# The sample stream's products with the old mLSTM memory: unsplit fp32, one key block per strip of 32 PSUM partitions

## The chip, the cores and the metric

The kernel runs on one core of one Trainium2 chip. The metric is the device time of one execution in microseconds (us). The time of a kernel is the median of its runs. Beside them one execution is profiled; times of single instructions, waits and windows come from that execution, counted from the start of its span.

## The reference

One layer of a streaming encoder is computed for a prompt of 512 frames and for a sample of 32 frames that continues a running stream. Two branches, an mLSTM with 4 heads of width 512 and an HGRN2 with 8 heads of width 128, are merged by gates and projected. The change lies in the mLSTM, in the term that reads the old matrix memory `C`, which only the sample has:

```python
s = jnp.einsum('bhtd,bhsd->bhts', q, k) * dmat
num = w_inter[..., None] * jnp.einsum('bhed,bhtd->bhte', C, q) + jnp.einsum('bhts,bhse->bhte', s, v)
den = w_inter * jnp.einsum('bhd,bhtd->bht', n, q) + jnp.sum(s, axis=-1)
h = num / jnp.maximum(jnp.abs(den), jnp.exp(-m_t))[..., None]
C_new = decay[..., None, None] * C + jnp.einsum('bhs,bhse,bhsd->bhed', w_last, v, k)
```

For the sample of one head, `num` is the product of 32 weighted queries (512 long) with a 512 x 512 memory, plus the 32 x 32 scores times the values. The kernel keeps the normaliser `n` as further columns of the memory, so that numerator and denominator come out of the same products, 516 columns wide (`VW`), in two halves of 258 (`VH`).

## The kernel before, in words

**Products.** Nearly all products are made from split operands: a value is stored as a high part in fp32r (a copy on ScalarE, ACT in the profile) and the rest as a low part (a subtraction on VectorE, DVE), and high x high, high x low and low x high are summed in PSUM. TensorE (PE) runs at one pass per such product. A few small products are left unsplit in fp32, those of the HGRN2 chain among them (L1511, L1606, L1630 to L1634).

**Order.** PE executes in the order in which the code is written. A generator `mchain(h, pump)` holds one mLSTM head's chain; at each `yield` it lets the `Pump` issue some of the products of the input projection (L370, L485), so that PE has work while the chain's results are copied. The orders of ACT and DVE are made by a scheduler from readiness and priority when the program is built; `tc.high_priority()` raises what it encloses. GpSimd (POOL) does small copies, SyncE (SP) issues loads and stores.

**One head in mchain.** Keys and values are transposed, weighted and split: `kw[b]` (high and low) and `vv[b]` for the four prompt blocks b, `kws` and `vs` for the sample. The old memory is loaded into `c0[f]`, f = 0 to 3 for the key blocks of 128 (L950). Then, in the order in which PE meets it:

- `old(f)` splits `c0[f]` into `c0h` and `c0l` (L956 on ACT, L957 on DVE).
- Heads 0 to 2: `memory(h, f, ...)` makes the prompt's new memory for f = 0 to 3, 24 products each (tile `C`, L902), and ACT copies each result out in two pieces (`Co`, L914). Behind each of them stands one `new_memory` product (tile `Cs`, L1004), which DVE merges into `c0` (L1006). In head 3 the operands are stored to `kv_d` instead, and the prompt's memory is made at the end of the program.
- The numerators `nm` of the prompt blocks i = 0 to 3 (L1077: 6, 12, 18 and 24 products), with the other `new_memory` products between them. Each result is copied out by ACT (`y`, L1088).
- Ahead of the last block, `sample()`: 16 split products with the old memory (L1054) and two with the scores (`dss`, L1051). The queries' high and low parts stand side by side in `qw`, so that PSUM partitions 0 to 31 receive the high and 32 to 63 the low part's sum; ACT copies the two out (L1063, L1065) and DVE adds them (L1066).

**Buffers.** The PSUM tiles of `paux` (`vt`, `vts`, `C`, `nm`, `yt`) come from a pool of two buffers, of two banks each. A new tile takes a buffer when the last reader of its former tile is done. `Cs` tiles come from another pool (`pd`) of four, which the projection shares. In SBUF there are 22 slots "s" and 12 slots "e" for tiles of 550 columns; `kw`, `vv` and the `y` tiles live in "s".

Of the kernel before, what the change touches and what calls it, by code (L numbers as in the profile page):

```python
# [9 lines left out]
F32 = mybir.dt.float32  # L10
F32R = mybir.dt.float32r
# [3 lines left out]
ALU = mybir.AluOpType  # L15
AX = mybir.AxisListType

P = 128
D = 1024
KD = D // P  # L20
NS = 32
# [5 lines left out]
KH = HD // P  # L27
HH = 8
NB = NP // P
VW = HD + 4  # L30
# [34 lines left out]
def hybrid_step(ctx: ExitStack, tc: tile.TileContext, a, o):  # L65
# [12 lines left out]
    def slot(name, dt=F32):  # L78
        return sp.tile([P, SLOT], dt, tag="s", name=name)
# [5 lines left out]
    def small(name, shape, dt=F32, bufs=2, tag=None):  # L85
        return tp.tile(shape, dt, tag=tag or name, name=name, bufs=bufs)

    def two(ap):
        return ap.rearrange("p (a b) -> p a b", a=2)
# [8 lines left out]
    def paux(name):  # L98
        return pa.tile([P, 2, 512], F32, tag="a", name=name)
# [724 lines left out]
    def stage_q(h, u):  # L824

        t = st8[h]
        if u == 0:
            t.update(qs=[], qf=small("qf", [P, KH * NS]), qw=small("qw", [P, KH, 2, NS], F32R))
        with tc.high_priority() if u and not h else nullcontext():
            w = t.pop("wq", None) or weight(a["w_qm"][h, u], f"wq{h}{u}")  # L830
        for f in range(2):
            acc = dense(w, f * P, 256, P, t["cs"], f"q{h}{u}{f}")
            i = u * 2 + f
            qh, ql = [eslot(f"q{n}{h}{i}", F32R) for n in "hl"] if h else pair_tile(f"q{i}", 1)
            S.copy(t["qf"][:, i * NS : (i + 1) * NS], acc[0][:, :NS])
            for b in range(2):
                with tc.high_priority():
                    read = S.copy(qh[:, half(b)], acc[b])
                    low = V.tensor_tensor(ql[:, half(b)], acc[b], qh[:, half(b)].bitcast(F32), ALU.subtract)
            t["qs"].append((qh, ql))  # L840
        if u:

            with tc.issue_after(read.ins):
                S.activation(small("silu", [1, 2]), ident[:1, :2], AF.Silu)
        return low

    def stage_scores(h):

        dj, ds, wi, ks, ksm, qs, qf, qw = (st8[h][k] for k in ("dj", "ds", "wi", "ks", "ksm", "qs", "qf", "qw"))
        for i in range(KH):  # L850
            qt = small("qt", [P, NS])
            G.tensor_tensor(qt, qf[:, i * NS : (i + 1) * NS], wi, ALU.mult)
            G.tensor_copy(qw[:, i, 0], qt)
            G.tensor_tensor(qw[:, i, 1], qt, qw[:, i, 0].bitcast(F32), ALU.subtract)
        sh2, sl2 = slot(f"sh2{h}", F32R), slot(f"sl2{h}", F32R)
        st = []
        for j in range(NB):
            pn = paux(f"sc{h}{j}")
            n = NP - j * P
            for f in range(KH):  # L860
                for i, (x, y) in enumerate(((0, 0), (0, 1), (1, 0))):
                    PE.matmul(  # L862
                        pn[:, 0, :n],
                        ks[f][x][:, j * P : (j + 1) * P],
                        qs[f][y][:, NS + j * P : T],
                        start=(f == 0 and i == 0),
                        stop=(f == KH - 1 and i == 2),
                    )
            with tc.high_priority():
                V.tensor_tensor(dj[j], pn[:, 0, :n], dj[j], ALU.mult)  # L870
            if j < 2:
                sh, sl = slot(f"sh{h}{j}", F32R)[:, :n], slot(f"sl{h}{j}", F32R)[:, :n]
            else:
                sh, sl = (x[:, (j - 2) * 256 : (j - 2) * 256 + n] for x in (sh2, sl2))
            with tc.high_priority():
                S.copy(sh, dj[j])  # L876
                low = V.tensor_tensor(sl, dj[j], sh.bitcast(F32), ALU.subtract)
            st.append((sh, sl))
        pn = paux(f"scs{h}")
        for f in range(KH):  # L880
            PE.matmul(
                pn[: 3 * NS, 0, :NS],
                ksm[:, f],
                qf[:, f * NS : (f + 1) * NS],
                start=(f == 0),
                stop=(f == KH - 1),
            )
        dss = small("dss", [3 * NS, NS], F32R)
        V.tensor_tensor(ds, pn[: 3 * NS, 0, :NS], ds, ALU.mult)
        V.tensor_copy(dss, ds)  # L890
        V.tensor_tensor(dss[2 * NS :], ds[2 * NS :], dss[2 * NS :].bitcast(F32), ALU.subtract)
        st8[h].update(st=st, dss=dss)
        return low
# [26 lines left out]
    def mchain(h, pump):  # L920
# [28 lines left out]
        for f in range(KH):  # L949
            nc.sync.dma_start(c0[f][:, :VW], a["C0"][h, f])  # L950

        def old(f):
            new = eslot if f < 2 else slot
            ch, cl = new(f"c0h{h}{f}", F32R), new(f"c0l{h}{f}", F32R)
            with tc.high_priority():
                S.copy(ch[:, :VW], c0[f][:, :VW])  # L956
                V.tensor_tensor(cl[:, :VW], c0[f][:, :VW], ch[:, :VW].bitcast(F32), ALU.subtract)  # L957
            return ch, cl


        if h:
            yield max(0, max(pump.when["v", f] for f in range(KH)) - pump.done)
        vt = t["vt"]
# [31 lines left out]
                for k in (1, 2):  # L995
                    xf[k] = xf_sums(k)
        yield 4
        olds = [old(0), old(1)]

        def new_memory(f, g):  # L1000

# [6 lines left out]
                nc.sync.dma_start(o["Cs"][h, f], c0[f][:, :VW])  # L1008

        parts = [(f, g) for f in range(KH) for g in range(2)]  # L1010
        if h == MH - 1:

            for b in range(NB):
                for i in range(2):
                    nc.sync.dma_start(kv_d[b, i, :, :HD], kw[b][i][:, :HD].bitcast(F32))
                    nc.sync.dma_start(kv_d[NB + b, i, :, :VW], vv[b][i][:, :VW].bitcast(F32))
        else:
            for f in range(KH):
                for _ in memory(h, f, kw, vv):
                    pass  # L1020
                new_memory(*parts.pop(0))


        st, dss, qw = (t[k] for k in ("st", "dss", "qw"))
        stt = small("stat", [P, NB + 1, 2])
        den = small("den", [P, NB + 1])
        emc = small("emc", [P, NB + 1])
# [6 lines left out]
        def numbers(i, p, y):  # L1034
            bs = small("bs", [P, 6])
            V.bn_stats(bs[:p], y[:p, :HD])  # L1036
            V.bn_aggr(stt[:p, i, :], bs[:p])
            V.tensor_copy(den[:p, i : i + 1], y[:p, HD : HD + 1])

        yb = []  # L1040
        olds += [old(2), old(3)]

        def sample():
            pn = paux(f"nm{h}{NB}")
            for f in (0, 1, 3, 2):
                ch, cl = olds[f]
                last = f == 2
                for g in range(2):
                    v = slice(g * VH, (g + 1) * VH)
                    if last:  # L1050
                        PE.matmul(pn[:NS, g, :VH], dss, vs[:, v], start=False, stop=False)  # L1051
                    both, low = (4 if last or f == 0 else 2, 0), (1, 1)
                    for m, x in (low, both) if last else (both, low):
                        PE.matmul(  # L1054
                            pn[: m * NS, g, :VH],
                            qw.rearrange("p f o t -> p (f o t)")[:, 2 * f * NS : (2 * f + m) * NS],
                            (ch, cl)[x][:, v],
                            start=(f == 0 and x == 0),
                            stop=(last and x == 0),
                        )  # L1060
            ysm = slot(f"y{h}{NB}")
            with tc.high_priority():
                S.copy(two(ysm[:, :VW]), pn[:, :, :VH])  # L1063
                yl = slot(f"yl{h}")
                S.copy(two(yl[:NS, :VW]), pn[NS : 2 * NS, :, :VH])  # L1065
                V.tensor_tensor(ysm[:NS, :VW], ysm[:NS, :VW], yl[:NS, :VW], ALU.add)  # L1066
                numbers(NB, NS, ysm)
            return ysm

        for i in range(NB):  # L1070
            if i == NB - 1:
                ysm = sample()
            pn = paux(f"nm{h}{i}")
            for j in range(i + 1):
                for q, (x, y) in enumerate(((0, 0), (0, 1), (1, 0))):
                    for g in range(2):
                        PE.matmul(  # L1077
                            pn[:, g, :VH],
                            st[j][x][:, (i - j) * P : (i - j + 1) * P],
                            vv[j][y][:, g * VH : (g + 1) * VH],  # L1080
                            start=(j == 0 and q == 0),
                            stop=(j == i and q == 2),
                        )
                if parts and i and (h == MH - 1 or i > 1):
                    new_memory(*parts.pop(0))
            y = slot(f"y{h}{i}")
            with tc.high_priority():
                S.copy(two(y[:, :VW]), pn[:, :, :VH])  # L1088
                numbers(i, P, y)
            yb.append(y)  # L1090
# [795 lines left out]
```

## Time and profile before

| | |
|---|---|
| time, median of 3 runs | 1140.07 us |
| the 3 runs | 1138.1, 1140.07, 1141.18 us |
| profiled execution, own time | 1136.01 us |
| its span, first to last instruction | 1134.3 us |
| PE busy | 1116.8 us (98%) |
| DVE busy | 896.5 us (79%) |
| ACT busy | 680.2 us (60%) |
| POOL busy | 185.9 us (16%) |
| granted TensorE clock | 1.00 of full |

The busy time of PE counts modelled ends of pipelined products, which overlap; the start of one product to the start of the next is what it costs. A row of the timeline gives start, duration, engine, line, operation, tiles written and read, the stationary operand as rows*columns, the output form, and how many were merged. In a row of the waits, PE is listed with what it sat idle for. The four heads' chains lie at about 104 to 165, 225 to 300, 388 to 445 and 540 to 605 us.

### The profile page before, as it was taken

The page shows a single profiled execution, that of the slowest core. Times are in us where ns is not written, and L with a number is a line of the kernel's source. Part 1 is how long each engine was busy: PE and PEld are TensorE (multiplying, and loading weights), DVE is VectorE, ACT ScalarE, POOL GpSimd, SP SyncE. Part 2 cuts the span into 40 slices and gives each one's busy share as a digit, 9 for nine tenths or more (in the row PEclk, how much of TensorE's full clock was granted, in tenths as well). Part 3 has the DMA queues.
Part 4 walks back from the last instruction along what each step waited for, and adds up shares of the span by engine and source line. Part 5 has one row for each costly group of instructions (what it writes and reads, how often), then busy time and mean ns, then how long its engine had stood idle before and what let it go on. Part 6 is the DMA issues. An engine that isn't in the chain of part 4 may idle for free.

```text
span 1134.3 us, 24068 instructions
## 1 busy us (share of the span) xinstructions
PE 1116.8 (98%) x8849; PEld 1101.4 (97%) x8849; DVE 896.5 (79%) x2027; ACT 680.2 (60%) x1537; POOL 185.9 (16%) x363
## 2 busy tenths in 40 slices
PE   9999999999999999999999999999999999999998
PEld 8999999999999999999999999999998999999998
DVE  6887998576896786976888699999999867654585
ACT  5677557655666555665665477677766657333462
POOL 4842010100010100101000122223232220000000
PEclk9999999999999999999999999999999999999999
DMA  7134224323344142552767766666666686332743
GB/s 236 56 96 133 79 75 159 118 95 106 132 152 151 49 131 105 158 168 69 239 163 234 180 145 143 138 140 140 148 149 165 174 222 172 113 103 70 269 141 116
DMA packets 91006, 159.68 MB, mean 141 GB/s; under 512 B 10245, under 2 KB 17797, under 8 KB 90889
## 3 DMA queue, kind: packets, MB, share of 16 engines
q1 hardware_dynamic: 80928, 140.27, 38.3%
q0 software_dynamic: 9792, 17.83, 10.1%
q8 instruction: 69, 1.13, 0.4%
q14 instruction: 49, 0.39, 0.1%
q10 hardware_dynamic: 168, 0.06, 0.0%
HBM read 133.21 MB, written 24.91 MB: 139 GB/s over the span
## 4 chain that ended last, share of the span: by engine, by line
PE 78%; DVE 10%; DMA 5%; ACT 3%; issue 2%; POOL 0%; SPq 0%; ACTq 0%; DVEq 0%
PE d L485 29%; PE ya L151 8%; PE pg L1736 4%; PE q L151 4%; PE yb L151 4%; PE o L151 4%; PE C L902 4%; PE k L151 4%; DMA ws<-in_w_in 3%; PE sc L862 3%; PE nm L1077 2%; PE pl L1511 2%; PE d L370 1%; DVE cv L634 1%; PE ple L151 1%
## 5 line engine op out<-in xcount | busy, mean ns | idle before, releaser
L403 POOL DMA_DIRECT2D ws<-in_w_in x46 | 40.3, 876 | 230.3 <-DVE rsq_u L168 30.3
L499 ACT COPY t<-d 128x272 f32<-128x272 f32 x126 | 47.7, 379 | 3.2 <-PE d L485 3.1
L1535 DVE TENSOR_TENSOR hkq<-hkq,q 128x288 f32<-128x288 f32 (+1 forms) x96 | 40.8, 432 | 3.9 <-PE pl L1519 1.0
L634 DVE SCALAR_TENSOR_TENSOR cv<-ub,vec,cv 128x547 f32<-128x547 f32 x48 | 40.4, 842 | 1.3 <-ACT cv L629 0.6
L1511 PE MATMUL pl<-hkq,km 128*128 128x128 f32 x224 | 38.0, 292 | 1.8 <-ACT km L1500 1.7
L1511 PEld LDWEIGHTS pl<-hkq,km 128*128 128x128 f32 x224 | 31.1, 189 | 3.9 <-ACT km L1500 3.4
L1500 ACT COPY km<-hkq 128x256 f32<-128x256 f32 x56 | 24.0, 428 | 15.6 <-DVE hkq L1535 6.2
L1006 DVE SCALAR_TENSOR_TENSOR c<-c,wi,Cs 128x258 f32<-128x258 f32 x32 | 15.3, 479 | 20.0 <-PE Cs L1004 19.8
L460 POOL DMA_DIRECT2D ws<-in_w_in x22 | 23.2, 1055 | 41.0 <-DVE ws272l L131 27.4
L914 ACT COPY Co<-C 128x258 f32<-128x258 f32 x32 | 10.4, 378 | 29.1 <-PE C L902 22.3
L1145 DVE TENSOR_TENSOR y<-ya,y 128x272 f32<-128x272 f32 x48 | 19.1, 436 | 10.3 <-PE ya L151 9.2
L1542 DVE COPY_PREDICATED at<-lmask,pl 128x256 f32<-128x256 uint8 (+1 forms) x56 | 25.3, 451 | 0.0
L1088 ACT COPY y<-nm 128x516 f32<-128x516 f32 x16 | 9.5, 591 | 21.6 <-PE nm L1077 21.5
L799 POOL COPY vsm<-vt 128x96 f32<-128x96 f32 x16 | 6.0, 382 | 88.2 <-ACT vt L510 44.7
L1479 POOL TENSOR_SCALAR_AFFINE_SELECT aa<-at 128x128 f32<-128x128 f32 x32 | 18.8, 621 | 8.9 <-DVE at L1542 8.9
L1077 PE MATMUL nm<-vhl,sh 128*128 128x258 f32 x112 | 18.3, 285 | 0.0
L1036 DVE BATCH_NORM_STATS2 bs<-y 128x6 f32<-128x512 f32 (+1 forms) x20 | 13.8, 688 | 5.5 <-ACT y L1088 5.5
L1723 DVE TENSOR_TENSOR h<-o,h 128x272 f32<-128x272 f32 x16 | 6.3, 436 | 14.5 <-PE o L151 14.5
L978 POOL CAST vhl<-one 128x4 fp32r<-128x4 f32 x8 | 2.0, 244 | 95.8 <-PE nm L1077 95.8
L876 ACT CAST sh<-dm 128x512 fp32r<-128x512 f32 (+3 forms) x16 | 7.3, 459 | 16.6 <-DVE dm L870 16.6
L1641 ACT ACTIVATE osq<-kq 128x128 f32<-128x128 f32 x32 | 9.8, 305 | 12.3 <-DVE kq L1636 12.1
L1710 DVE TENSOR_TENSOR gb<-yb,gb 128x272 f32<-128x272 f32 x16 | 6.3, 436 | 13.1 <-PE yb L151 13.1
(4490 smaller groups left out, 5072.9 us busy)
## 6 DMA issues: line engine op xcount, KB each, us to landing
ws<-in_w_in POOLq DMA_DIRECT2D x68, 256.0 KB, 4.8
ws<-in_w_in SPq DMA_DIRECT2D x46, 256.0 KB, 3.6
ya_d<-y SPq DMA_DIRECT2D x32, 272.0 KB, 2.7
y<-ya_d SPq DMA_DIRECT2D x24, 272.0 KB, 3.7
c<-in_C SPq DMA_DIRECT2D x16, 258.0 KB, 3.9
out_Cp<-Co SPq DMA_DIRECT2D x16, 258.0 KB, 2.5
out_Cs<-c SPq DMA_DIRECT2D x16, 258.0 KB, 2.8
x<-in_xT SPq DMA_DIRECT2D x8, 272.5 KB, 4.7
```

The source lines that it names most:

```text
L151: PE.matmul(both[b][:m, :TH], part(w, off + k * step, m, x), xx[:, half(b)], start=(k == 0 and j == 0), stop=(k == n - 1 and j == 2),)
L403: G.dma_start(t, w_in[u][:, i * WP : (i + 1) * WP], accum_op=ALU.add)
L485: PE.matmul(ps, ww[:, c], xx, start=(start and k == 0 and j == 0), stop=end, skip_group_check=not start,)
L499: S.copy(t, ps)
L634: V.scalar_tensor_tensor(cv[:, :547], ub[:, j : j + 547], vcol(V_CW + 4 * ft + j), cv[:, :547], ALU.mult, ALU.add)
L862: PE.matmul(pn[:, 0, :n], ks[f][x][:, j * P : (j + 1) * P], qs[f][y][:, NS + j * P : T], start=(f == 0 and i == 0), stop=(f == KH - 1 and ...
L902: PE.matmul(pn[g][:, :VH], kw[b][x][:, f * P : (f + 1) * P], vv[b][y][:, g * VH : (g + 1) * VH], start=(b == 0 and j == 0), stop=(b == NB ...
L1077: PE.matmul(pn[:, g, :VH], st[j][x][:, (i - j) * P : (i - j + 1) * P], vv[j][y][:, g * VH : (g + 1) * VH], start=(j == 0 and q == 0), stop ...
L1511: PE.matmul(pn[:, 0, b * P : (b + 1) * P], km[:, b * P : (b + 1) * P], view(qq, b * P, ((2 * c, P // (2 * c)), (HB + c, 2), (1, c))), star ...
L1535: V.tensor_tensor(x, x, d, ALU.mult)
L1542: V.copy_predicated(at[:, :n], lmask[:, li, :n], pn[:, 0, :n])
L1736: PE.matmul(ps, part(w, k * P, P, x), xx[:, c], start=(k == 0 and j == 0), stop=(k == KD - 1 and j == 2))
```

## The change

The split of the old memory and of the weighted queries goes. `qw` holds unsplit fp32 queries. `sample()` multiplies each key block's 32 queries with `c0[f]` as one fp32 product per half, into its own strip of 32 PSUM partitions, and adds the scores' product to strip 0. ACT copies all four strips out, and DVE adds three of them to the first. The call moves ahead of the prompt's memory products.

```diff
-            t.update(qs=[], qf=small("qf", [P, KH * NS]), qw=small("qw", [P, KH, 2, NS], F32R))
+            t.update(qs=[], qf=small("qf", [P, KH * NS]), qw=small("qw", [P, KH, NS]))
...
-            qt = small("qt", [P, NS])
-            G.tensor_tensor(qt, qf[:, i * NS : (i + 1) * NS], wi, ALU.mult)
-            G.tensor_copy(qw[:, i, 0], qt)
-            G.tensor_tensor(qw[:, i, 1], qt, qw[:, i, 0].bitcast(F32), ALU.subtract)
+            G.tensor_tensor(qw[:, i], qf[:, i * NS : (i + 1) * NS], wi, ALU.mult)
...
-        def old(f):
-            new = eslot if f < 2 else slot
-            ch, cl = new(f"c0h{h}{f}", F32R), new(f"c0l{h}{f}", F32R)
-            with tc.high_priority():
-                S.copy(ch[:, :VW], c0[f][:, :VW])
-                V.tensor_tensor(cl[:, :VW], c0[f][:, :VW], ch[:, :VW].bitcast(F32), ALU.subtract)
-            return ch, cl
...
         yield 4
-        olds = [old(0), old(1)]
...
         parts = [(f, g) for f in range(KH) for g in range(2)]
+        st, dss, qw = (t[k] for k in ("st", "dss", "qw"))
+
+        def sample():
+            pn = paux(f"nm{h}{NB}")
+            for g in range(2):
+                v = slice(g * VH, (g + 1) * VH)
+                for f in range(KH):
+                    PE.matmul(pn[f * NS : (f + 1) * NS, g, :VH], qw[:, f], c0[f][:, v], start=True, stop=f > 0)
+                PE.matmul(pn[:NS, g, :VH], dss, vs[:, v], start=False, stop=True)
+            ysm = slot(f"y{h}{NB}")
+            with tc.high_priority():
+                S.copy(two(ysm[:, :VW]), pn[:, :, :VH])
+                for f in range(1, KH):
+                    yl = slot(f"yl{h}{f}")
+                    S.copy(two(yl[:NS, :VW]), pn[f * NS : (f + 1) * NS, :, :VH])
+                    V.tensor_tensor(ysm[:NS, :VW], ysm[:NS, :VW], yl[:NS, :VW], ALU.add)
+            return ysm
+
+        ysm = sample()
         if h == MH - 1:
...
         yb = []
-        olds += [old(2), old(3)]
-
-        def sample():
...
+        numbers(NB, NS, ysm)
         for i in range(NB):
-            if i == NB - 1:
-                ysm = sample()
             pn = paux(f"nm{h}{i}")
```

What the built programs show of the order: first ACT in head 0, where the sample's result (`y04`, `yl`) and the prompt's memories (`Co`) are copied out. Numbers behind a name are the head and the block, those behind the underline tell tiles apart; a wait is shown with the engine whose count it waits for. Before, the sample's copies stood behind the numerators of three prompt blocks:

```order
L914 COPY Co03_1986<-C03_1961 128x258 [waits DMAHW0_49,PE_49,Activation_49]
L914 COPY Co03_1986<-C03_1961 128x258
L321 CAST xfh2_1808<-xv20_1811 128x272 [waits DVE_49]
L1088 COPY y00_2017<-nm00_2010 128x516 [waits PE_49]
L1088 COPY y01_2036<-nm01_2023 128x516 [waits PE_49]
L1088 COPY y02_2071<-nm02_2042 128x516 [waits PE_49]
L1063 COPY y04_2096<-nm04_2077 128x516 [waits PE_49]
L1065 COPY yl0_2098<-nm04_2077 32x516 [waits Activation_49]
L1088 COPY y03_2134<-nm03_2105 128x516 [waits PE_49]
```

Now the same place:

```order
L911 COPY Co02_1956<-C02_1931 128x258 [waits PE_49]
L911 COPY Co02_1956<-C02_1931 128x258
L1009 COPY y04_1855<-nm04_1844 128x516 [waits PE_49,Activation_49]
L1012 COPY yl01_1857<-nm04_1844 32x516 [waits PE_49]
L1012 COPY yl02_1860<-nm04_1844 32x516 [waits PE_49,Activation_49]
L1012 COPY yl03_1863<-nm04_1844 32x516 [waits PE_49]
L911 COPY Co03_1988<-C03_1963 128x258 [waits PE_49]
L911 COPY Co03_1988<-C03_1963 128x258
L1063 COPY y00_2015<-nm00_2008 128x516 [waits PE_49,Activation_49]
```

The sample's products have moved ahead of all four memories on PE, but its four copies stand behind the copies of three of them on ACT. They need "s" slots: the count that `y04` waits for is that of the fourth product of `C03`, the last reader of `kwh00`, whose slot `y04` takes.

Second, PE in head 0. Before, from the first `Cs` to the third memory:

```order
L1004 MATMUL Cs000_1893<-vs_1786,kws_1681 128x258 [waits DVE_49]
L902 MATMUL C01_1896<-vhl00_1703,kwh00_1615 128x258 [waits PE_49]
...
L1004 MATMUL Cs001_1925<-vs_1786,kws_1681 128x258
L902 MATMUL C02_1929<-vhl00_1703,kwh00_1615 128x258 [waits Activation_49]
...
L1004 MATMUL Cs010_1958<-vs_1786,kws_1681 128x258 [waits DVE_49]
```

Now, from the sample's last product on:

```order
L1006 MATMUL nm04_1844<-vs_1774,dss_1546 32x258
L899 MATMUL C00_1866<-vhl00_1691,kwh00_1603 128x258 [waits PE_49]
...
L991 MATMUL Cs000_1895<-vs_1774,kws_1669 128x258
L899 MATMUL C01_1898<-vhl00_1691,kwh00_1603 128x258 [waits Activation_49]
...
L991 MATMUL Cs001_1927<-vs_1774,kws_1669 128x258
L899 MATMUL C02_1931<-vhl00_1691,kwh00_1603 128x258 [waits Activation_49]
...
L899 MATMUL C03_1963<-vhl00_1691,kwh00_1603 128x258 [waits Activation_49]
```

Before, the memories alternated between the two PSUM buffers, and the wait of `C02` for ACT was for the copy of `C00`, made a memory earlier. Now the sample's tile holds one of the two, and `C00` to `C03` all stand in the other: `C01` waits for the second copy of `C00`, `C02` for that of `C01`, `C03` for that of `C02`. Heads 1 and 2 read the same.

More of the change, by code (lines that the diff above doesn't have):

```diff
@@ L1021, in mchain @@
                 new_memory(*parts.pop(0))
-        st, dss, qw = (t[k] for k in ("st", "dss", "qw"))
         stt = small("stat", [P, NB + 1, 2])
@@ L1040, in mchain @@
         yb = []
-        olds += [old(2), old(3)]
-        def sample():
[L1044 to L1068, printed above, removed]
+        numbers(NB, NS, ysm)
         for i in range(NB):
-            if i == NB - 1:
-                ysm = sample()
             pn = paux(f"nm{h}{i}")
```

## Prediction

> **What bounds the kernel now.** I read the page's first part, then the busy time by windows over the four heads, then the waits of PE.
>
> ```profile
> PE 1116.8 (98%) x8849; PEld 1101.4 (97%) x8849; DVE 896.5 (79%) x2027; ACT 680.2 (60%) x1537; POOL 185.9 (16%) x363
> ```
> ```profile
> 104.00:165.00 61.00, 60.03 (x490) 58.87 (x489) 58.14 (x153) 34.68 (x68) 5.54 (x19) 1.00 0.25 83
> 225.00:300.00 75.00, 74.77 (x595) 73.61 (x594) 55.02 (x119) 40.33 (x83) 5.07 (x24) 1.00 0.28 94
> 540.00:605.00 65.00, 63.38 (x504) 61.99 (x504) 58.15 (x127) 42.70 (x80) 7.06 (x14) 1.00 0.64 193
> ```
> ```profile
> PE d L485 <- ACT t L499: 2.5, 2, 1.6
> PE Cs L1004 <- DVE c L1006: 1.0, 3, 0.5
> ```
>
> The columns behind the window's length are PE, weight loads, DVE, ACT, POOL. PE is busy for nearly all of each head (74.77 of 75 us in head 1), and over the whole program the largest single group of its idle time is 2.5 us. DVE comes close in head 0 (58.14 of 61) and head 3 (58.15 of 65) only. So PE sets the pace: what lengthens or pauses PE's row shows in the time, and what other engines save doesn't.
>
> **The change part by part.** The sample's products first, in head 0 before:
>
> ```profile
> 139.89 0.28 PE L1054 MATMUL nm<-c0h,qw 128*128 128x258 f32 x1
> 140.01 0.28 PE L1054 MATMUL nm<-c0l,qw 128*32 128x258 f32 x1
> 140.12 0.28 PE L1054 MATMUL nm<-c0h,qw 128*128 128x258 f32 x1
> ...
> 141.91 0.28 PE L1054 MATMUL nm<-c0h,qw 128*128 128x258 f32 x1
> 142.03 0.63 PE L1077 MATMUL nm<-vhl,sh 128*128 128x258 f32 x4
> ```
>
> Eighteen products from 139.89 to 142.03: 2.14 us, 0.119 each. They go, and 8 fp32 products and two like the old ones (0.24 us) come. What an unsplit product costs is seen in the HGRN2 chain:
>
> ```profile
> L1511 PE MATMUL pl<-hkq,km x224: 272/282/386, 645.4 to 884.4; 128*128 128x128 f32 x112
> ```
> ```profile
> 672.15 0.39 PE L1632 MATMUL ho<-tf,hkq 128*128 128x128 f32 x2
> 672.37 0.39 PE L1630 MATMUL ho<-hi,aa 128*128 128x128 f32 x2
> ...
> 673.49 0.39 PE L1634 MATMUL ho<-s,hkq 128*128 128x128 f32 x2
> ```
>
> The code makes 8 x 7 x 2 = 112 products at L1511 and the trace has 224 rows: each unsplit product is two passes. Six products start between 672.15 and 673.49, 0.223 us apart for 128 columns; for 258 columns that gives 0.450 us, two passes of 0.225. No row shows products into different strips, so I bound it from both sides. If strips run one after another, 8 x 0.450 + 0.24 = 3.84 us, 1.70 more than before in each head, 6.8 in all. If the four strips of a half run together, 2 x 0.450 + 0.24 = 1.14 us, 1.0 less per head, 4.0 less in all. Between them: products start in order, the second pass of a strip needs the place of its first pass, and only the first pass of the next strip can run beside it. Four strips then take five passes instead of eight, 1.13 us a half, the scores' product beside the last of them: 2.2 us, as much as before. I take this one, because the passes of every unsplit product above follow in pairs, and no row shows one overtaking another.
>
> The Trainium skill (TensorE: Matmul & The Clock Gate, Measured speedup) has three column strips run 2.38 times as fast as one by one; by it the eight would take an estimated 3.60/2.38 = 1.5 us, and the sum below would come out 1.8 us lower. No row here can show it. The same rows bear on another of its rules: in the old sample stationary operands 128 and 32 columns wide alternate at the pitch of 0.119. The Trainium skill (TensorEngine Tiling (Array Packing), Key Properties) says that changing the tiling mode drains TensorE; by that the old sample would hold a drain at each alternation, which the new one would save. The rows show none, so nothing is taken off.
>
> Next, the PSUM buffers: this is the term that decides. With the sample's tile held until ACT has copied it out, behind `Co02`, the memories of heads 0 to 2 share one buffer, and each of C1, C2, C3 starts only when both copies of the one ahead are done. Copy and resumption stand in the trace:
>
> ```profile
> 125.83 0.28 PE L1004 MATMUL Cs<-vs,kws 96*128 96x258 f32 x1
> 125.95 0.64 PE L902 MATMUL C<-vhl,kwh 128*128 128x258 f32 x4
> 134.86 0.30 PE L1004 MATMUL Cs<-vs,kws 96*128 96x258 f32 x1
> 134.99 0.65 PE L1077 MATMUL nm<-vhl,sh 128*128 128x258 f32 x4
> 135.48 0.40 PE L1077 MATMUL nm<-vhl,sl 128*128 128x258 f32 x2
> 135.81 0.75 PE L1077 MATMUL nm<-vhl,sh 128*128 128x258 f32 x4
> 136.39 0.40 PE L1077 MATMUL nm<-vhl,sl 128*128 128x258 f32 x2
> ```
> ```profile
> 126.03 0.65 ACT L914 COPY Co<-C 128x258 f32<-128x258 f32 x2 [1.74 <-PE C L902]
> 135.10 0.65 ACT L914 COPY Co<-C 128x258 f32<-128x258 f32 x2 [0.21 <-PE C L902]
> 142.23 0.59 ACT L1063 COPY y<-nm 128x516 f32<-128x516 f32 x1 [1.68 <-PE nm L1054]
> 142.85 0.58 ACT L1065 COPY yl<-nm 32x516 f32<-32x516 f32 x1
> ```
>
> The copies begin 0.20 to 0.24 us after `Cs` starts and take 0.65. At 135.75 the fourth memory is copied out, and at 135.81 the numerator that waits for that buffer starts: 0.06 later. So C1 can start 0.24 + 0.65 + 0.06 = 0.95 us after `Cs`, where now 0.12 pass (125.83 to 125.95): a pause of 0.83. The four products behind such a wait took 0.58 us (135.81 to 136.39) and without one 0.49 (134.99 to 135.48), 0.09 for a weight load that nothing covers. Each pause costs 0.92, nine of them 8.3 us. On ACT nothing is in the way: it sat idle for 1.74 us ahead of the first copy.
>
> The sample's four copies then fall into C3. The first waits for C3's fourth product, some 0.8 us into it, and four at the pitch of 142.23 to 142.85 (0.62) end at 3.2, where the numerators want the buffer at 3.1 (24 products, one `Cs` and the load). That costs 0.2, about what the wait at 135.81 costs before, which goes; I count the two as equal.
>
> Head 3 has no memories here. There its second numerator takes the sample's buffer and waits for all four copies. The first copy starts 0.32 us after the sample's last product (141.91 to 142.23), four end 2.77 after it, and with 0.06 and the load of 0.09 the numerator starts at 2.92, where six products of the first numerator would have let it start at 0.12 + 0.72 = 0.84: a pause of 2.1. Against it stands a wait of before in that place, which goes, because DVE has no `c0l` left to make:
>
> ```profile
> 571.07 0.40 PE L1077 MATMUL nm<-vhl,sl 128*128 128x258 f32 x2
> 571.99 0.39 PE L1004 MATMUL Cs<-vs,kws 96*128 96x258 f32 x1 [0.52 <-DVE c L1006]
> ```
>
> That is 0.5, so head 3 loses 1.6 us.
>
> What is taken off the other engines:
>
> ```profile
> L956 ACT CAST c0h<-c x16: 607/622/633, 116.5 to 569.4; 128x516 fp32r<-128x516 f32 x16
> L957 DVE TENSOR_TENSOR c0l<-c,c0h x16: 686/690/699, 118.0 to 570.8; 128x516 fp32r<-128x516 f32 x16
> L1066 DVE TENSOR_TENSOR y<-y,yl x4: 676/690/726, 143.6 to 578.7; 32x516 f32<-32x516 f32 x4
> L854 POOL TENSOR_TENSOR qw<-qt,qw x16: 247/254/587, 96.3 to 527.0; 128x32 fp32r<-128x32 f32 x16
> ```
>
> ACT loses 16 x 0.62 and gains 8 x 0.58, DVE loses 16 x 0.69 and gains 8 x 0.69, or 5.5 us; POOL loses 32 operations of a quarter of a us. I cost all of it at nothing, since PE is busy over it; were DVE to set the pace, it would be a gain of up to 5.5.
>
> Last, new waits ahead of the sample on PE, behind which all of PE's row would queue: the loaded memory and `vs`.
>
> ```profile
> 550.73 2.88 SPq L950 DMA_DIRECT2D c<-in_C  x4
> ```
> ```profile
> c<-in_C SPq DMA_DIRECT2D x16, 258.0 KB, 3.9
> ```
> ```profile
> L992 DVE TENSOR_TENSOR vs<-vts,vs x4: 683/683/684, 120.9 to 567.2; 32x512 fp32r<-32x512 f32 x4
> ```
> ```profile
> 569.01 0.64 PE L1077 MATMUL nm<-vhl,sh 128*128 128x258 f32 x4
> ```
>
> In head 3 the loads are issued by 553.6 and land 3.9 us later, `vs` is done at 567.9, and the place at which the sample will stand is reached at 569.01. Both cost nothing.
>
> Sum: 8.3 + 1.6 + 4 x (2.2 - 2.14) = 10.1 us on PE's row. On the profiled execution (1136.01, span 1134.3) that is 1146; the median of the runs shown lies 4 us above that execution, and the forecast is made on it: 1140.07 + 10 = 1150.
>
> **The rivals.** *Strips one after another* (chance 0.29): the same pauses, and 6.8 - 0.2 us more: 1157. For it: no row shows two products side by side. Against it: nothing either.
>
> *All four together* (0.13): 1140 + 8.3 + 1.6 - 4.0 = 1146. Against it: two passes per product, issued in order.
>
> *DVE sets the pace, so that pauses of PE are covered* (0.08): the 5.5 us that DVE loses come off, 1134.5, faster than before. For it: DVE's share in heads 0 and 3. It decides when, in these heads, PE waits for DVE for longer than the pauses, 9.9 us; the waits of before show 1.0 us at `Cs` in all. Against it, head 1 with DVE at 55.02 of 75.
>
> *The pauses don't come about or are given back* (0.05): the change would do on PE what it says and no more, 1140. It needs ACT to copy the sample out ahead of `Co00`, and ACT's order is fixed when the program is built.
>
> **How the numbers follow.** The likeliest case (0.45) gives 1150. The range takes in the cases on both sides with their own rounding, 1144 to 1158, and leaves out the last two. A measurement of this kernel can tell about 0.3% (3.4 us) from no change: three cases lie above 1143.5 (0.87), one in between (0.05), one below (0.08).
>
> **What would show it.** PE's waits should have a new group, `C` (L899) behind the copies of `Co` (L911), nine times at some 0.8 us, and one of about 2 us of `nm` in head 3 behind the sample's last copy. The sample's ten products from first to last tell the cases apart: 1.1, 2.2 or 3.8 us. The forecast is wrong if `C01` starts beside `Co00`, or if waits of PE for DVE or ACT elsewhere shrink by as much as the pauses add.

## The result, and the profile after

The changed kernel takes 1148.29 us (median of four runs, 1145.71 to 1149.80) against 1140.61 us for the kernel before on the same chip: a ratio of 1.0068, with a 95% interval of 1.0049 to 1.0087. That is 7.7 us more, 5.6 to 9.9 by the interval. Forecast were 1150, 1144 to 1158, and slower.

The two profiled executions lie further apart than the medians: spans of 1146.5 and 1134.3 us. Of these 12.2 us, 4.5 stand at one late place, to which the last section comes back.

The page's first part, of the changed kernel, and then its waits of PE (engine and line, released by; us in all, times, longest):

```profile
PE 1120.9 (98%) x8849; PEld 1098.5 (96%) x8849; DVE 891.7 (78%) x2019; ACT 677.4 (59%) x1529; POOL 178.3 (16%) x331
```
```profile
PE C L899 <- ACT Co L911: 5.9, 9, 0.7
PE d L485 <- ACT t L499: 3.6, 2, 2.7
PE nm L1052 <- ACT yl L1012: 1.8, 1, 1.8
...
PE Cs L991 <- DVE c L993: 0.6, 2, 0.3
```

The first and the third group are new: nine waits of the memories for the copies of the memory ahead, and one of 1.8 us in head 3 behind the sample's last copy. DVE has 4.8 us less to do than before, and nothing of that shows in the time.

PE's timeline of the changed kernel in head 0 (start, duration, and behind the row the idle time and what ended it): the sample, the end of `C00`, `C01`.

```profile
123.07 0.64 PE L1005 MATMUL nm<-c,qw 128*32 128x258 f32 x8
123.64 0.31 PE L1006 MATMUL nm<-vs,dss 96*32 96x258 f32 x1
123.88 0.64 PE L1005 MATMUL nm<-c,qw 128*32 128x258 f32 x8
124.45 0.30 PE L1006 MATMUL nm<-vs,dss 96*32 96x258 f32 x1
124.59 0.64 PE L899 MATMUL C<-vhl,kwh 128*128 128x258 f32 x4
...
127.48 0.28 PE L991 MATMUL Cs<-vs,kws 96*128 96x258 f32 x1
128.38 0.75 PE L899 MATMUL C<-vhl,kwh 128*128 128x258 f32 x4 [0.62 <-ACT Co L911]
128.97 0.40 PE L899 MATMUL C<-vhl,kwl 128*128 128x258 f32 x2
```

The sample takes 1.52 us (123.07 to 124.59), 0.62 less than before and less than the 2.2 forecast. Between `Cs` and the second memory pass 0.90 us in place of 0.12, and the four products behind the wait take 0.59 in place of 0.48: a pause of head 0 costs 0.89. In heads 1 and 2 it is a little more (PE's timeline of the changed kernel, head 1):

```profile
276.22 0.28 PE L991 MATMUL Cs<-vs,kws 96*128 96x258 f32 x1
277.18 0.74 PE L899 MATMUL C<-vhl,kwh 128*128 128x258 f32 x4 [0.68 <-ACT Co L911]
277.76 0.41 PE L899 MATMUL C<-vhl,kwl 128*128 128x258 f32 x2
```

Here 0.96 us pass in place of 0.12, and the four products take 0.58: 0.94. Three pauses of 0.89 and six of 0.94 make 8.3 us.

ACT's timeline of the changed kernel at the same place shows why the buffer is held so long:

```profile
127.68 0.65 ACT L911 COPY Co<-C 128x258 f32<-128x258 f32 x2 [0.19 <-PE C L899]
...
131.57 0.65 ACT L911 COPY Co<-C 128x258 f32<-128x258 f32 x2 [2.40 <-PE C L899]
...
135.46 0.65 ACT L911 COPY Co<-C 128x258 f32<-128x258 f32 x2 [0.31 <-PE C L899]
136.99 0.59 ACT L1009 COPY y<-nm 128x516 f32<-128x516 f32 x1 [0.89 <-PE C L899]
137.61 1.80 ACT L1012 COPY yl<-nm 32x516 f32<-32x516 f32 x3
```

The sample's tile is full at 124.6, and its copies run from 136.99 to 139.41. ACT idles for 2.40 us in between: it isn't short of time, its copy is short of an SBUF slot.

In head 3 the second numerator waits for all four copies (PE's timeline of the changed kernel):

```profile
577.87 0.64 PE L1052 MATMUL nm<-vhl,sh 128*128 128x258 f32 x4
578.35 0.40 PE L1052 MATMUL nm<-vhl,sl 128*128 128x258 f32 x2
580.53 0.75 PE L1052 MATMUL nm<-vhl,sh 128*128 128x258 f32 x4 [1.78 <-ACT yl L1012]
```

Where the difference stands behind the four heads is read from one group of the numerators' tile, in the kernel before and in the changed one (fastest, median and slowest ns of one; first and last start):

```profile
L1077 PE MATMUL nm<-vh,sl x24: 278/282/294, 139.5 to 580.7; 128*128 128x258 f32 x24
```
```profile
L1052 PE MATMUL nm<-vh,sl x24: 276/282/293, 143.9 to 589.2; 128*128 128x258 f32 x24
```

The last numerators start 8.5 us later. What the change costs is spent by then.

### The profile page after: what moved, and what is told of

It is laid out like the page before. It is cut to its first block, busy times and chain, and to the rows that moved or that the text cites. A ratio compares the mean times of both kernels' runs of the same rounds, so it can differ in the third digit from the quotient of the medians.

```text
span 1146.5 us, 24041 instructions
## 1 busy us (share of the span) xinstructions
PE 1120.9 (98%) x8849; PEld 1098.5 (96%) x8849; DVE 891.7 (78%) x2019; ACT 677.4 (59%) x1529; POOL 178.3 (16%) x331
## 3 DMA queue, kind: packets, MB, share of 16 engines
q0 software_dynamic: 9792, 17.83, 10.1%
## 4 chain that ended last, share of the span: by engine, by line
PE 71%; DVE 12%; DMA 7%; ACT 5%; issue 3%; POOL 1%; SPq 0%; ACTq 0%; DVEq 0%; POOLq 0%
PE d L485 24%; PE ya L151 8%; DMA ws<-in_w_in 5%; PE C L899 4%; PE pg L1711 4%; PE q L151 4%; PE yb L151 4%; PE o L151 4%; PE k L151 4%; PE sc L859 3%; PE nm L1052 2%; PE pl L1486 1%; PE d L370 1%; DVE cv L634 1%; PE ple L151 1%
## 5 line engine op out<-in xcount | busy, mean ns | idle before, releaser
L1120 DVE TENSOR_TENSOR y<-ya,y 128x272 f32<-128x272 f32 x48 | 19.0, 435 | 10.1 <-PE ya L151 9.1
L899 PE MATMUL C<-vhl,kwh 128*128 128x258 f32 x96 | 16.4, 292 | 5.9 <-ACT Co L911 5.9
L899 PEld LDWEIGHTS C<-vhl,kwh 128*128 128x128 f32 x96 | 13.1, 190 | 7.8 <-ACT Co L911 7.8
L626 POOL COPY uo<-ub 128x3 f32<-128x3 f32 x16 | 12.3, 767 | 39.7 <-DVE ub L508 28.3
L1052 PEld LDWEIGHTS nm<-vhl,sh 128*128 128x128 f32 x112 | 15.4, 190 | 2.6 <-ACT yl L1012 2.6
```

The source lines that it names most:

```text
L899: PE.matmul(pn[g][:, :VH], kw[b][x][:, f * P : (f + 1) * P], vv[b][y][:, g * VH : (g + 1) * VH], start=(b == 0 and j == 0), stop=(b == NB ...
L1052: PE.matmul(pn[:, g, :VH], st[j][x][:, (i - j) * P : (i - j + 1) * P], vv[j][y][:, g * VH : (g + 1) * VH], start=(j == 0 and q == 0), stop ...
```

## The experiments

Eight kernels were run, each against the kernel before on the same chip. All are edits of the changed kernel. First, whether the held PSUM buffer costs the time, and what holds it.

**The copies in another pool.** The four copies go into buffers of the pool `eslot`, so that they needn't wait for the readers of old `slot` buffers.

```diff
-            ysm = slot(f"y{h}{NB}")
+            ysm = eslot(f"y{h}{NB}")
...
-                    yl = slot(f"yl{h}{f}")
+                    yl = eslot(f"yl{h}{f}")
```

> The four copies of the sample's tile go into buffers of another SBUF pool, so that they no longer wait for the readers of the numerators' old buffers, and ACT copies them ahead of Co00. Theory (the pauses at the held PSUM buffer are the loss): the nine waits of C behind Co, 5.9 us by the waits of the changed kernel and about 0.87 each with the slower start behind them, 7.9 in all, are gone; the sample's 0.6 us per head stays gained. The four copies, 2.4 us, now stand ahead of Co00 on ACT, which may pause C02 once per head by up to 2 us, 6 in all, if C02 needs the sample's buffer before the copies are done. 1148.3 - 7.9 = 1140.4, up to 1146 with that wait; the wait group of C behind Co falls from nine entries to three at the most. Rival (the loss sits further back, in the wait for t ahead of the d products and the lower granted clock behind it, or in the place of the sample): removing the pauses brings under 3 us, 1146 or more, with the wait group gone.

Measured: 1137.53 us against 1140.02, ratio 0.9981 (0.9969 to 0.9993). The waits of PE have no group of `C` behind `Co` any more; in head 3 a shorter wait stands, at a later numerator:

```profile
PE nm L1052 <- ACT y L1063: 1.2, 1, 1.2
```

So with all nine pauses gone the kernel is 2.5 us faster than before (0.8 to 3.5 by the interval). The rival that puts the loss further back falls. The feared wait at `C02` did not come.

The shorter sample alone would give as much (4 x 0.62), but the wait of 1.2 us in head 3 comes off that, so the match is luck. In the two profiles the last numerators start only 0.2 us earlier than in the kernel before (580.5 against 580.7):

```profile
L1052 PE MATMUL nm<-vh,sl x24: 277/282/292, 141.2 to 580.5; 128*128 128x258 f32 x24
```

From the changed kernel's 7.7 us more to these 2.5 less it is 10.2 us. The nine pauses (8.3) and the shorter wait in head 3 (1.2 for 1.8) make 8.9 of them, which the two intervals allow.

**One copy out of PSUM.** As above, and the strips are taken out of the SBUF copy:

```diff
-                    yl = slot(f"yl{h}{f}")
-                    S.copy(two(yl[:NS, :VW]), pn[f * NS : (f + 1) * NS, :, :VH])
+                    yl = eslot(f"yl{h}{f}")
+                    S.copy(yl[:NS, :VW], ysm[f * NS : (f + 1) * NS, :VW])
```

> As the run with the other pool, and the three strips are then taken out of the SBUF copy of the tile and no longer out of PSUM: the PSUM buffer is free after one copy of 0.6 us in place of four in 2.4. Theory: no wait of C behind Co is left, and head 3's pause of 2.0 us falls to 0.3 or less. With the sample's 1.52 us against 2.14 before, four times: before - 2.5, and up to 0.5 more for the wait at Cs that is gone: 1137 to 1138, faster than both kernels. Rival (the loss sits elsewhere): 1146 or more. Second rival (the pauses go, but the longer way of the strips, four copies one behind the other and an add each, reaches y's normalisation later than PE needs it): 1140 to 1143 and a new wait of PE behind DVE or ACT at the end of each head.

Measured: 1136.54 us against 1140.02, ratio 0.9970 (0.9957 to 0.9983): 3.5 us less, so it beats both kernels. No wait of `C` or `nm` is left among the waits of PE, nor a new one behind DVE at the end of a head; the second rival falls too. In its profile the last numerators start 0.6 us earlier than before; where the rest of the 3.5 us comes from is not shown.

**Late copies with the buffer held, and with the buffer free.** The two runs above also move copies on ACT to an earlier place. This pair keeps the strips late in both kernels. In the first, only the strips' source changes: they are read from the SBUF copy, which itself stays late. In the second, one buffer more goes to the other pool, so that this one copy runs at once.

```diff
 first:
-                    S.copy(two(yl[:NS, :VW]), pn[f * NS : (f + 1) * NS, :, :VH])
+                    S.copy(yl[:NS, :VW], ysm[f * NS : (f + 1) * NS, :VW])
 second, beside that:
-            ysm = slot(f"y{h}{NB}")
+            ysm = eslot(f"y{h}{NB}")
```

> Only the strips' source differs from the changed kernel: they are taken out of the SBUF copy. The copy of the sample's tile itself keeps its late SBUF buffer and stands behind Co02 as before, so the PSUM buffer is held as long. Theory (the hold makes the pauses): nine waits of C behind Co stay, about 0.87 us each; only head 3 gains, since its second numerator waits for one copy and not four: 2.0 us less, of which up to 1.2 may come back at the third numerator, whose buffer waits for a copy behind the strips on ACT: 1146.3 to 1147.5. Rival (four long copies out of PSUM are what disturbs, not the hold): 1140 or less.

> The partner of the run with the late, held buffer: one buffer goes to the other SBUF pool, the one for the copy of the sample's tile, so that this one copy runs at once and frees PSUM; the strips are still late, behind Co02, and as many. Theory (the hold): the nine waits are gone, 7.9 us less than its partner: 1137 to 1139. Rival (the late copies and sums themselves cost): as its partner, 1146 or more.

Measured on one chip, against 1140.66: the first 1145.35 us, ratio 1.0046 (1.0034 to 1.0058); the second 1137.32 us, ratio 0.9973 (0.9961 to 0.9984). They are 8.0 us apart, where the nine pauses make 8.3. ACT's timeline in head 0, the first kernel's and then the second's:

```profile
137.25 0.59 ACT L1009 COPY y<-nm 128x516 f32<-128x516 f32 x1 [0.89 <-PE C L899]
137.88 1.92 ACT L1012 COPY yl<-y 32x516 f32<-32x516 f32 x3
```
```profile
124.44 0.59 ACT L1009 COPY y<-nm 128x516 f32<-128x516 f32 x1 [0.85 <-PE nm L1006]
...
134.36 1.92 ACT L1012 COPY yl<-y 32x516 f32<-32x516 f32 x3
```

And PE's, the first kernel's and the second's:

```profile
127.74 0.28 PE L991 MATMUL Cs<-vs,kws 96*128 96x258 f32 x1
128.64 0.75 PE L899 MATMUL C<-vhl,kwh 128*128 128x258 f32 x4 [0.62 <-ACT Co L911]
```
```profile
127.13 0.29 PE L991 MATMUL Cs<-vs,kws 96*128 96x258 f32 x1
127.25 0.64 PE L899 MATMUL C<-vhl,kwh 128*128 128x258 f32 x4
```

The strips and their sums are late in both, and cost nothing that shows: the second kernel's ratio of 0.9973 can't be told apart from the 0.9970 of the kernel in which they are early. The place of one copy decides: at 124.44 it frees the buffer before the second memory asks for it. The first kernel has also lost the wait of 1.8 us in head 3, since the second numerator waits there for one copy instead of four. Its median is 2.9 us below that of the changed kernel and below the 1146.3 to 1147.5 expected; each was compared with other runs of the kernel before, and the two intervals overlap. In the profiles its last numerators start 1.5 us earlier (587.7 against 589.2).

Next, what made the sample short.

**One strip.** All four key blocks accumulate in the first 32 partitions, with one copy out and no sums:

```diff
-                    PE.matmul(pn[f * NS : (f + 1) * NS, g, :VH], qw[:, f], c0[f][:, v], start=True, stop=f > 0)
+                    PE.matmul(pn[:NS, g, :VH], qw[:, f], c0[f][:, v], start=f == 0, stop=False)
...
```

> The change without its strips: all four key blocks accumulate in the first 32 partitions, one copy out, no sums afterwards. The PSUM buffers are shared as in the changed kernel, so the nine pauses stay. Theory (strips run side by side and that is what made the sample short): eight products one behind the other at 0.45 us and the scores' two at 0.12 give 3.84 us per head against 1.52, 9.3 us more; in head 3 one copy in place of four shortens the pause by about 1.8: 1148.3 + 9.3 - 1.8 = 1155.8. Rival (the short sample comes from something else than the strips, for instance fp32 passes at twice the pace for 32 columns of qw): the sample stays at 1.5 us, 1146.5.

Measured: 1155.08 us against 1140.02, ratio 1.0133 (1.0117 to 1.0149).

**Two strips.** Key blocks 0 and 2 accumulate in one strip, 1 and 3 in the next; one strip is summed afterwards.

```diff
-                    PE.matmul(pn[f * NS : (f + 1) * NS, g, :VH], qw[:, f], c0[f][:, v], start=True, stop=f > 0)
+                    r = f % 2 * NS
+                    PE.matmul(pn[r : r + NS, g, :VH], qw[:, f], c0[f][:, v], start=f < 2, stop=f == 3)
...
```

> Two strips in place of four: key blocks 0 and 2 accumulate in the first 32 partitions, 1 and 3 in the next, so one strip is summed afterwards. The held buffer stays, and the nine pauses with it. Theory (products of different strips run side by side, those of one strip one after another at 0.23 us a pass): a half takes 4 x 0.23 = 0.93 and its scores' product 0.24, 2.35 us for the sample against 1.52: 3.3 more in four heads; head 3 waits for two copies in place of four, 1.2 less: 1148.3 + 3.3 - 1.2 = 1150.4. Rival (accumulation in one strip, not the strip itself, is what made one strip slow): here the second product of a strip accumulates too, so near the 4.09 of one strip, 1157.

Measured: 1149.93 us against 1140.66, ratio 1.0080 (1.0065 to 1.0095). The rival's 1157 is not met: accumulation in a strip is not what made one strip slow.

**Key blocks outside, halves inside.** The same products as in the changed kernel, in another order:

```diff
-            for g in range(2):
-                v = slice(g * VH, (g + 1) * VH)
-                for f in range(KH):
+            for f in range(KH):
+                for g in range(2):
+                    v = slice(g * VH, (g + 1) * VH)
...
-                PE.matmul(pn[:NS, g, :VH], dss, vs[:, v], start=False, stop=True)
+            for g in range(2):
+                PE.matmul(pn[:NS, g, :VH], dss, vs[:, g * VH : (g + 1) * VH], start=False, stop=True)
```

> The same products in another order: both halves of one key block, in one strip, and then the next strip. Everything else stays. Theory 1 (strips run side by side only when neighbouring products go to different strips, pass by pass): now two neighbours share a strip, the overlap falls to that of one pair's end with the next pair's start, 0.45 x 8 less three or so overlapped passes of 0.225, about 3 us per head against 1.52: +6 us, 1154. Theory 2 (PE looks further ahead, any products to free strips overlap): 1.5 us, 1148.3.

Measured: 1145.97 us against 1140.02, ratio 1.0053 (1.0035 to 1.0071); from the changed kernel's ratio this can't be told apart.

PE's timeline in head 0 answers for the three: with one strip, with two, and with the blocks outside (the lines of the code shift by one or two).

```profile
123.69 1.93 PE L1005 MATMUL nm<-c,qw 128*32 128x258 f32 x8
125.55 0.30 PE L1006 MATMUL nm<-vs,dss 96*32 96x258 f32 x1
...
127.78 0.65 PE L899 MATMUL C<-vhl,kwh 128*128 128x258 f32 x4
```
```profile
123.69 1.06 PE L1006 MATMUL nm<-c,qw 128*32 128x258 f32 x8
124.68 0.30 PE L1007 MATMUL nm<-vs,dss 96*32 96x258 f32 x1
...
126.05 0.65 PE L899 MATMUL C<-vhl,kwh 128*128 128x258 f32 x4
```
```profile
122.83 1.10 PE L1005 MATMUL nm<-c,qw 128*32 128x258 f32 x16
123.86 0.42 PE L1007 MATMUL nm<-vs,dss 96*32 96x258 f32 x2
124.12 0.65 PE L899 MATMUL C<-vhl,kwh 128*128 128x258 f32 x4
```

| kernel | a half's products, to the scores' product | whole sample |
|---|---|---|
| one strip | 1.86 us (123.69 to 125.55) | 4.09 us |
| two strips | 0.99 us (123.69 to 124.68) | 2.36 us |
| four strips, the change | 0.57 us (123.07 to 123.64) | 1.52 us |
| four strips, blocks outside | 1.03 us for both halves (122.83 to 123.86) | 1.29 us |

Eight passes in one strip take 1.86 us, 0.23 each; in two strips they stand in four places, in four strips in two. So the strips run side by side, and each place costs about a pass. With the blocks outside, the first four passes in the program's order all belong to one strip. If a later product could not start ahead of an earlier one, the sixteen passes would take thirteen places, each strip's first pass beside the last of the strip ahead: 3 us. They took 1.03 us, so a strip's passes wait only for their own strip.

The one strip's time also bounds what strips are worth in this kernel: without them, unsplit products are slower than the old split ones (4.09 against 2.14 us).

**One copy, and blocks outside.** Both improvements together:

> The kernel with one copy out of PSUM, with the products in block-outer order. In the changed kernel that order took the ten products from 1.52 to 1.29 us (122.83 to 124.12 in head 0), since sixteen passes stood in four groups without the scores' product between the halves. Theory: 4 x 0.23 less than the kernel with one copy: 1136.5 - 0.9 = 1135.6, the fastest. Rival (the products' order matters only behind a pause): no gain, 1136.5.

```diff
-            for g in range(2):
-                v = slice(g * VH, (g + 1) * VH)
-                for f in range(KH):
+            for f in range(KH):
+                for g in range(2):
+                    v = slice(g * VH, (g + 1) * VH)
...
-            ysm = slot(f"y{h}{NB}")
+            ysm = eslot(f"y{h}{NB}")
...
-                    yl = slot(f"yl{h}{f}")
-                    S.copy(two(yl[:NS, :VW]), pn[f * NS : (f + 1) * NS, :, :VH])
+                    yl = eslot(f"yl{h}{f}")
+                    S.copy(yl[:NS, :VW], ysm[f * NS : (f + 1) * NS, :VW])
```

Measured: 1136.93 us against 1140.66, ratio 0.9977 (0.9963 to 0.9990). The sample takes 1.29 us here too (PE's timeline, head 0):

```profile
123.46 1.10 PE L1005 MATMUL nm<-c,qw 128*32 128x258 f32 x16
```

The 0.9 us that it should bring lie inside the interval of either kernel, so the time shows no gain and excludes none. The rows do show it: in the kernel with one copy, and then in this one, the last numerators start at 580.1 and at 579.2.

```profile
L1052 PE MATMUL nm<-vh,sl x24: 278/282/292, 141.4 to 580.1; 128*128 128x258 f32 x24
```
```profile
L1053 PE MATMUL nm<-vh,sl x24: 278/283/292, 141.4 to 579.2; 128*128 128x258 f32 x24
```

By the times the kernel with one copy stays the better supported version. The unsplit products at the sample's old place, behind the memories, were not run.

## Why the prediction was right

The sum was 10.1 us; 7.7 were measured. Its steps, one by one:

- *Nine pauses, 8.3 us.* Right in kind, number, place and size: 0.89 us each in head 0 and 0.94 in heads 1 and 2, 8.3 in all. The weight load that nothing covers was 0.1 as taken; in head 0 the copy began a little sooner behind `Cs` (0.20 us). The pair with the buffer held and free gave 8.0.
- *Head 3, 2.1 less 0.5.* The second numerator starts 2.66 us after the first (577.87 to 580.53), where it took 0.84 in the kernel with one late copy: 1.8. The waits at `Cs` went from 1.0 us to 0.6 in all, a little less than forecast.
- *The sample as long as before.* This step failed. "The second pass of a strip needs the place of its first pass, and only the first pass of the next strip can run beside it" took the pairs of the HGRN2 chain for a rule of issue; those pairs share their output columns, and say nothing of products that don't. All four strips go side by side, pass by pass. That was the rival *all four together*: its 1.14 us for the sample took 0.45 us for a half's products and 0.12 for the scores' product behind them, where 0.57 (123.07 to 123.64) and 0.24 in the first half, 0.57 and 0.14 in the second were measured, 1.52 in all. In the sum it is 2.5 us less than before where 0.2 more stood.
- *DVE, ACT and POOL at nothing.* Right: DVE lost 4.8 us, and in the kernels without the pauses the last numerators start 0.2 to 1.6 us earlier than before, no more than the shorter sample accounts for (2.5).

With the sizes measured, 8.3 + 1.8 - 0.4 - 2.5 make 7.2, inside the measured interval of 5.6 to 9.9. The forecast came out near because the step that failed was the smaller one. The 1148.3 us lie about as far from the 1146 of *all four together* as from the 1150 forecast: the time alone doesn't tell the two apart, the sample's rows do. The Trainium skill (TensorE: Matmul & The Clock Gate, Measured speedup vs the span model) would have brought the sample nearer: it has three column strips run 2.38 times as fast as one by one, and here two strips are 1.9 times as fast (1.86 over 0.99) and four 3.3 times (1.86 over 0.57). The prediction had cited it, with an estimate of 1.5 us for the eight products, and set it aside.

## What to carry to other kernels

Moving work ahead of its neighbours also moves the moment at which its buffers are taken, while the moment at which they come free is set by the slowest thing their reader waits for: look there first, here an SBUF slot held by an unrelated product 12 us later. If a PSUM tile has several readers, copy it out once into a buffer that is free, and let the rest read the copy. A rule about overlap read from instructions that share a resource can't be carried to instructions that don't; measure those in the arrangement that is meant.

## What the runs showed of the hardware

Strips of 32 output columns each keep their own order: in the blocks-outside kernel products of different strips passed each other, since sixteen passes took 1.03 us where the order of the program would take 3 (thirteen places of 0.23).

The granted clock fell to half behind some of PE's waits. At one late place PE waits for ACT. The windows of the changed kernel (10 us, and 2 of them), and then of the kernel with the late copies and the free buffer (length; busy times and counts by engine; then the granted clock, DMA's share and GB/s):

```profile
930.00:940.00 10.00, 8.71 (x47) 8.71 (x48) 5.22 (x9) 4.29 (x9) 1.72 (x3) 0.66 0.67 148
932.00:934.00 2.00, 2.00 (x11) 2.00 (x11) 0.69 (x1) 0.62 (x1) 0.00 (x0) 0.50 0.84 199
```
```profile
920.00:930.00 10.00, 9.49 (x75) 9.49 (x76) 6.77 (x12) 5.95 (x13) 1.75 (x2) 1.00 0.65 168
```

The first row of PE's timeline behind that wait, in the changed kernel, in that kernel, in the one with two strips, and in the kernel before:

```profile
931.29 0.60 PE L485 MATMUL d<-xfh,ws384h 128*128 128x272 f32 x1 [2.67 <-ACT t L499]
```
```profile
920.51 0.40 PE L485 MATMUL d<-xfh,ws384h 128*128 128x272 f32 x1 [2.54 <-ACT t L499]
```
```profile
934.27 0.39 PE L485 MATMUL d<-xfh,ws384h 128*128 128x272 f32 x1 [2.38 <-ACT t L499]
```
```profile
921.30 0.39 PE L485 MATMUL d<-xfh,ws384h 128*128 128x272 f32 x1 [1.62 <-ACT t L499]
```

A mean of 0.66 over 10 us is 6.8 us at half clock, which costs 3.4 us; with the 1.1 us more of wait (2.67 against 1.62) that makes 4.5, as much as the two spans' 12.2 us exceed the medians' 7.7. The median of the kernel before lies above its profiled execution, which had no such stretch. Of the ten profiles, the six with such a stretch had waits of 2.38 to 3.03 us at this place, the four without had 1.24 to 2.54. The Trainium skill (TensorE: Matmul & The Clock Gate, What's actually happening) has the clock halved after an idle window of about 3.4 us that runs on by itself. Here waits shorter than that sufficed, and their length alone did not decide. This stretch stands some 340 us behind the last numerators, and the kernel with one copy has it too and is the fastest. Whether the change makes it more frequent stays open: the changed kernel's four runs were granted 0.996 to 0.998 of the clock, the 38 runs of the kernel before beside the experiments 0.996 to 1.000, and so were the 21 runs of the four kernels that keep all nine pauses.
